# Differential projections ahead of the latent ones, and the output product of a hybrid attention block in Strassen's form

## The chip, the cores and the metric

One core of one Trainium2 chip runs the whole program. The metric is the device time of one execution in microseconds; the time of the kernel before is the median of three runs, 897.6 us (897.48 to 898.41).

## The reference

One decoder block over 1024 tokens with 1024 channels, all in float32. The input is normalised and projected; four heads of differential attention (two softmax maps, one subtracted from the other) and four heads of latent attention (queries and keys through low-rank projections) run on the same projection. What the change touches is the end:

```
merged = (jax.nn.sigmoid(g_diff) * (o_diff @ w_proj_diff[layer])
          + jax.nn.sigmoid(g_mla) * (o_mla @ w_proj_mla[layer]))
x = x + merged @ w_out[layer]
return rms_norm(x, norm_final)
```

Here `o_diff` and `o_mla` are 1024 x 512, the two projections 512 x 1024, `w_out` 1024 x 1024.

## The kernel before

Every product is made of matmuls on operands that are split in two parts, a rounded high part and the remainder as low part, so that a product of two float32 matrices is three matmuls of 512 columns (`mm3`, lines 159 to 162: high x high, high x low, low x high). `split` (lines 151 to 153) makes the two parts: a cast on ACT, then a subtraction on DVE or POOL.

The work is written down by Python generators. A generator yields the time that TensorE is thought to need; `fill`, `drain` and `drive` put pieces of one queue of generators between the steps of another, and `defer` and `flush` call a function once so many nanoseconds have been written down. From this order, the tiles' buffers and its own estimate of when an instruction can start, the framework sets each engine's final order: an instruction that it thinks is not yet ready is passed by later ones that are. On the chip each engine then takes its list strictly in that order, and SP's list of DMA issues too. A tile's buffer (a tag with so many `bufs`) is handed on when its last reader is through. PSUM has eight banks: four for scores, one each for `pv` and `tp`, and two under the tag `mm`, which the projections, the merge products and two of three transposes of the latent heads' values share (`tp_any`, line 760).

Ahead of the change stand the latent heads, h = 0 to 3, each with two groups of 512 queries: scores, softmax, transposes of the probabilities, values. Their loop is in lines 1030 to 1066. The places that the change touches are these.

- `merge_begin` (line 966) is called when head 2 is through. It opens the pool `p3a`, loads the four blocks of the differential output from `d_od` through one buffer of 128 x 1024 ("or"), splits each into `odh` and `odl` (line 974), and calls `load_p` twice.
- `load_p` (line 982) loads the next block of a projection weight (two buffers) and splits it with POOL; `p3["plan"]` holds their order.
- `product(br, j, done)` (line 995) is one merge product: for block j of 128 output channels and both halves of 512 tokens, 12 matmuls into a bank `mm`; branch 0 is differential, branch 1 latent. The gate's half tile `tg` is loaded from `d_t` (three buffers). `done_d` (line 1011) keeps the gated differential result in a tile `part`; `done_m` (line 1015) adds the latent one to it and splits the sum into `mh[j]`, `ml[j]`.
- When head 3 begins, pool `p3b` opens and products (0,0) and (0,1) are queued; `take` (line 1056) loads the latent output from `d_om` by halves through three buffers "omr" and splits it. These products stand between the steps of the last values, `mla_values(3, 1)`.
- Then products (1,j) and (0,j+2) alternate for j = 0 to 5, and (1,6), (1,7) follow (lines 1092 to 1096). `begin_out` loads and splits the first three blocks of `w_out`; the other five are loaded and split within the output stage.
- The output stage (line 1127 on) runs over the 8 blocks k of inner channels for the first four row blocks and both column halves, all eight banks in use, and then over row blocks 4 to 7 one at a time. `finish_half` adds the residual `x` and sums squares, `finish` scales the rows and stores them. The last row block is done in a half and two quarters of the columns, so that its finishing is short.

Of the kernel before, what the change touches and what calls it, by code (L numbers as in the profile page):

```python
# [23 lines left out]
P = 128  # L24
# [27 lines left out]
def emit(tc, a):  # L52
# [106 lines left out]
    def mm3(ps, lh, ll, rh, rl, first, last):  # L159
        T.matmul(ps, lhsT=lh, rhs=rh, start=first, stop=False)  # L160
        T.matmul(ps, lhsT=lh, rhs=rl, start=False, stop=False)  # L161
        T.matmul(ps, lhsT=ll, rhs=rh, start=False, stop=last)  # L162
# [801 lines left out]
    p3 = {}  # L964

    def merge_begin():
        pa = p3["a"] = pool("p3a", "right")
        p3["o"] = [[], []], [[], []]
        for k in range(4):
            r = mk(pa, [P, S], F32, "or", 1)  # L970
            nc.sync.dma_start(r, d_od[k])
            h_ = one(pa, [P, S], F32R, f"odh{k}")
            l_ = one(pa, [P, S], F32R, f"odl{k}")
            split(h_, l_, r)
            p3["o"][0][0].append(h_)
            p3["o"][0][1].append(l_)
        p3["w"] = deque()
        p3["plan"] = deque([(0, 0), (0, 1)] + [x for j in range(6) for x in ((1, j), (0, j + 2))] + [(1, 6), (1, 7)])
        for _ in range(2):
            load_p()  # L980

    def load_p():
        if p3["plan"]:
            br, j = p3["plan"].popleft()
            pa = p3["a"]
# [9 lines left out]
    def product(br, j, done):  # L995
        wh, wl = p3["w"].popleft()
        oh, ol = p3["o"][br]
        for n in range(2):
            t = mk(p3["a"], [P, 512], F32, "tg", 3)
# [30 lines left out]
    for h in range(4):  # L1030
# [17 lines left out]
        else:  # L1048
            pl2.release()
            pb = p3["b"] = pool("p3b", "right")  # L1050
            p3["o"][1][0].extend(one(pb, [P, S], F32R, f"omh{k}") for k in range(4))
            p3["o"][1][1].extend(one(pb, [P, S], F32R, f"oml{k}") for k in range(4))
            queue.append(product(0, 0, done_d))
            queue.append(product(0, 1, done_d))

            def take(k, n):
                r = mk(pb, [P, 512], F32, "omr", 3)
# [12 lines left out]

    p3c = pool("p3c", "left")
    mh = [one(p3c, [P, S], F32R, f"mh{j}") for j in range(8)]
    ml = [one(p3c, [P, S], F32R, f"ml{j}") for j in range(8)]
    EARLY = 3
    p3e = pool("p3e", "left")
    woh = [one(p3e, [P, D], F32R, f"woh{k}") for k in range(EARLY)]
    wol = [one(p3e, [P, D], F32R, f"wol{k}") for k in range(EARLY)]

    def load_out(k):
        wr = mk(p3e, [P, D], F32, "wor", 2)  # L1080
        nc.sync.dma_start(wr, a["w_out"][k])
        return wr

    def begin_out():
        raws = [load_out(k) for k in range(2)]
        split(woh[0], wol[0], raws[0])
        raws.append(load_out(2))
        split(woh[1], wol[1], raws[1])
        split(woh[2], wol[2], raws[2])

    defer(35000, begin_out)
    for j in range(6):
        queue.append(product(1, j, done_m))
        queue.append(product(0, j + 2, done_d))
    for j in (6, 7):
        queue.append(product(1, j, done_m))
# [3 lines left out]
    p3["a"].release()  # L1100

    p3d = pool("p3d", "right")
    nf = one(p3d, [P, D], F32, "nf")
    woh += [one(p3d, [P, D], F32R, f"woh{k}") for k in range(EARLY, KD)]
    wol += [one(p3d, [P, D], F32R, f"wol{k}") for k in range(EARLY, KD)]

    def load_res(b):
        xr = mk(p3d, [P, D], F32, "xres", 4)
        nc.sync.dma_start(xr, a["x"][b])
        return xr  # L1110

    def finish_half(xr, acc, s_, d):
        V.tensor_tensor(xr[:, half(d)], xr[:, half(d)], acc, op=ALU.add)
        junk = mk(p3d, [P, 512], BF16, "junk3", 1)
        A.activation(junk, xr[:, half(d)], AF.Square, accum_out=s_[:, d:d + 1])
        if d == 0:
            V.tensor_scalar(s_[:, 0:1], s_[:, 0:1], D * EPS, None, op0=ALU.add)

    def finish(b, xr, s_):
# [7 lines left out]
    ps.release()  # L1127
    ps3 = pool("ps3", space=PSUM)
    acc = [[mk(ps3, [P, 512], F32, "acc", 8) for d in range(2)] for q in range(4)]
    wos = deque(load_out(k) for k in (3, 4))  # L1130
    nc.sync.dma_start(nf, a["norm_final"].broadcast_to([P, D]))
    for k in range(KD):
        if k + 1 >= EARLY and k + 1 < KD:
            split(woh[k + 1], wol[k + 1], wos.popleft())
            if k + 3 < KD:
                wos.append(load_out(k + 3))
        for q in range(4):
            for d in range(2):
                mm3(acc[q][d], mh[k][:, blk(q)], ml[k][:, blk(q)], woh[k][:, half(d)], wol[k][:, half(d)],
                    k == 0, k == KD - 1)  # L1140
    res = [load_res(q) for q in range(4)]
    for q in range(4):
        s_ = mk(p3d, [P, 2], F32, "s3", 4)
        for d in range(2):
            finish_half(res[q], acc[q][d], s_, d)
        finish(q, res[q], s_)
    for b in range(4, NB - 1):
        xr = load_res(b)
# [111 lines left out]
```

## Time and profile before

| | |
|---|---|
| median of three runs | 897.6 us |
| the profiled execution's own time | 896.13 us |
| its span, first to last instruction | 894.4 us |
| between the two | 1.7 us |
| mean granted clock of TensorE | 0.995 |
| TensorE busy | 874.7 us, 98% |
| DVE, ACT, POOL busy | 538.5, 335.5, 219.5 us |

The page lists, for one profiled execution, how long each engine was busy, and 40 slices of the span. Times in the rows below are microseconds from the span's start. Durations of matmuls overlap (the next one starts before the last has drained), so the pace of TensorE is read from the distance of starts. A bracket at the end of a row tells how long the engine had stood before it and on what it waited.

### The profile page before, as it was taken

How to read it: one execution, taken by the hardware profiler on the slowest of the kernel's cores; microseconds unless marked ns; L12 is line 12 of the kernel's file. 1: busy time of each engine (PE TensorE's matmuls, PEld its weight loads, DVE VectorE, ACT ScalarE, POOL GpSimd, SP SyncE). 2: the span in 40 equal slices, each digit the busy share in tenths (PEclk: the TensorE clock that was granted, in tenths of full speed). 3: DMA queues.
4: the chain of work that ended last, by engine and by line, in shares of the span. 5: the costliest groups of instructions: out<-in, count | busy, mean ns of one | idle time of the engine just before them, and what ended most of it. 6: DMA issues, size and time to landing. Idle time of an engine off the chain costs nothing.

```text
span 894.4 us, 11691 instructions
## 1 busy us (share of the span) xinstructions
PE 874.7 (98%) x4368; PEld 716.0 (80%) x4368; DVE 538.5 (60%) x1023; ACT 335.5 (38%) x654; POOL 219.5 (25%) x163
## 2 busy tenths in 40 slices
PE   9989999999999999999999999999999999999997
PEld 6879988787887878878778778778877788888886
DVE  5472348738368483784856755786676775561432
ACT  5651361334323343233422333745455542221211
POOL 2432013222223222322223131622313212210001
PEclk9998999999999999999999999999999999999999
DMA  8765026122131222222211215410104655434151
GB/s 294 289 192 161 23 87 220 48 71 80 62 107 59 76 90 64 91 71 82 72 59 33 95 31 185 161 34 25 48 25 154 200 178 187 141 102 146 58 178 47
DMA packets 48824, 96.71 MB, mean 108 GB/s; under 512 B 4992, under 2 KB 17536, under 8 KB 48768
## 3 DMA queue, kind: packets, MB, share of 16 engines
q1 hardware_dynamic: 46176, 89.81, 30.4%
q0 software_dynamic: 1152, 3.67, 1.3%
q10 hardware_dynamic: 1440, 2.49, 0.8%
q8 instruction: 34, 0.56, 0.3%
q14 instruction: 22, 0.18, 0.1%
HBM read 68.96 MB, written 27.00 MB: 107 GB/s over the span
## 4 chain that ended last, share of the span: by engine, by line
PE 85%; DVE 4%; DMA 4%; issue 2%; ACT 2%; POOL 1%; SPq 1%; POOLq 0%; DVEq 0%; ACTq 0%
PE mm L160 18%; PE mm L162 17%; PE mm L161 17%; PE sc L619 4%; PE acc L160 3%; PE acc L161 3%; PE acc L162 3%; PE tp L457 2%; PE bank L161 2%; PE bank L160 2%; PE bank L162 2%; PE pv L161 2%; PE pv L160 2%; PE pv L162 1%; PE sc L898 1%
## 5 line engine op out<-in xcount | busy, mean ns | idle before, releaser
L160 PE MATMUL mm<-hh,wh 128*128 128x512 f32 x512 | 205.9, 402 | 0.0
L162 PE MATMUL mm<-hh,wl 128*128 128x512 f32 x512 | 200.2, 391 | 0.0
L161 PE MATMUL mm<-hl,wh 128*128 128x512 f32 x512 | 199.9, 390 | 0.0
L153 POOL TENSOR_TENSOR wl<-wr,wh 128x1024 fp32r<-128x1024 f32 x32 | 81.8, 2558 | 240.2 <-ACT wh L152 240.2
L160 PEld LDWEIGHTS mm<-hh,wh 128*128 128x128 f32 x512 | 96.2, 188 | 25.0 <-issue 3.8
L162 PEld LDWEIGHTS mm<-hh,wl 128*128 128x128 f32 x512 | 96.1, 188 | 21.2
L161 PEld LDWEIGHTS mm<-hl,wh 128*128 128x128 f32 x512 | 96.3, 188 | 17.9
L438 ACT ACTIVATE e<-sc,mn 128x128 f32<-128x128 f32 (+3 forms) x64 | 47.5, 743 | 82.9 <-DVE mn L435 80.0
L435 DVE CUSTOM_DVE_ANT_0 sc<-sc,mask 128x128 f32<-128x128 f32 (+7 forms) x96 | 71.7, 774 | 10.1 <-PE sc L902 8.7
L153 DVE TENSOR_TENSOR pl<-tp,ph 128x512 fp32r<-128x512 f32 (+2 forms) x52 | 31.5, 606 | 62.2 <-ACT ph L152 62.2
L152 ACT CAST ph<-tp 128x512 fp32r<-128x512 f32 (+2 forms) x52 | 27.0, 520 | 84.7 <-PE tp L457 84.2
L160 PE MATMUL acc<-woh,mh 128*128 128x512 f32 (+1 forms) x136 | 51.7, 380 | 0.0
L162 PE MATMUL acc<-woh,ml 128*128 128x512 f32 (+1 forms) x136 | 51.7, 380 | 0.0
L161 PE MATMUL acc<-wol,mh 128*128 128x512 f32 (+1 forms) x136 | 51.7, 380 | 0.0
L152 ACT CAST wh<-wr 128x1024 fp32r<-128x1024 f32 x32 | 33.6, 1050 | 39.0 <-PE mm L161 28.6
L160 PE MATMUL bank<-wch,hh 128*128 128x384 f32 (+1 forms) x128 | 42.7, 335 | 3.8 <-ACT wch L152 3.8
L911 POOL TENSOR_TENSOR e<-e,rs 128x128 f32<-128x128 f32 (+5 forms) x24 | 24.9, 1042 | 73.5 <-DVE rs L443 73.4
L161 PE MATMUL bank<-wcl,hh 128*128 128x384 f32 (+1 forms) x128 | 42.6, 333 | 0.3 <-DVE wcl L153 0.3
L569 DVE TENSOR_TENSOR g<-mm,rbc 128x512 f32<-128x512 f32 x40 | 27.5, 688 | 25.5 <-PE mm L162 25.0
L162 PE MATMUL bank<-wch,hl 128*128 128x384 f32 (+1 forms) x128 | 42.4, 331 | 0.0
L153 POOL TENSOR_TENSOR wpl<-wpr,wph 128x512 fp32r<-128x512 f32 x16 | 22.0, 1377 | 68.0 <-ACT wph L152 68.0
L572 ACT ACTIVATE u<-g 128x512 f32<-128x512 f32 x40 | 25.2, 630 | 20.3 <-DVE g L569 15.4
(291 smaller groups left out, 1859.0 us busy)
## 6 DMA issues: line engine op xcount, KB each, us to landing
wr<-in_w_t SPq DMA_DIRECT2D x32, 512.0 KB, 3.5
d_t<-u SPq DMA_DIRECT2D x32, 256.0 KB, 2.0
tg<-d_t SPq DMA_DIRECT2D x32, 256.0 KB, 3.0
big<-in_x SPq DMA_DIRECT2D x8, 512.0 KB, 8.3
wor<-in_w_out SPq DMA_DIRECT2D x8, 512.0 KB, 4.5
xres<-in_x SPq DMA_DIRECT2D x8, 512.0 KB, 5.1
big<-in_xT SPq DMA_DIRECT2D x7, 512.0 KB, 6.6
craw<-d_c SPq DMA_DIRECT2D x5, 512.0 KB, 6.0
```

The costliest lines, as they stand in the source:

```text
L152: A.copy(hi, src)
L153: (eng or V).tensor_tensor(lo, src, f32(hi), op=ALU.subtract)
L160: T.matmul(ps, lhsT=lh, rhs=rh, start=first, stop=False)
L161: T.matmul(ps, lhsT=lh, rhs=rl, start=False, stop=False)
L162: T.matmul(ps, lhsT=ll, rhs=rh, start=False, stop=last)
L435: V.tensor_tensor_reduce(sc[:, 0:W], sc[:, 0:W], mask[:, S - W:S], scale=-scale, scalar=BIG, op0=ALU.add, op1=ALU.min, accum_out=mn)
L438: A.activation(dst, sc[:, 0:W], AF.Exp, scale=-1.0, bias=mn, accum_out=sm)
L457: T.transpose(tp[:, blk(j)], probs[j][:, blk(kb)], ident)
L569: V.tensor_tensor(g, b, rbc[:, half(n)], op=ALU.mult)
L572: A.activation(u, g, AF.Tanh, scale=0.5 / by)
L619: T.matmul(sc[m][:, c0:c0 + n], lhsT=q[r, blk(i)], rhs=k[r, c0:c0 + n], start=x == 0, stop=x == 2)
L911: G.tensor_tensor(e, e, r.broadcast_to([P, W]), op=ALU.mult)
```

## The change

The latent and differential merge products no longer alternate: all eight differential ones come first, in the order of blocks 0, 4, 1, 5, 2, 6, 3, 7 (`JO`), then the eight latent ones in the same order. Pool `p3b` is opened already in `merge_begin`, and holds the latent output, the weights, the gates, `omr` (two buffers instead of three) and four `part` tiles; `p3a` holds only the differential output, which is now loaded in eight halves through one buffer of 128 x 512. `p3a` is given back between the two series. The merged matrix stays unsplit in `mr[j]`.

The output product is made as seven products of 512 x 512 x 512 (Strassen's form with Winograd's sums). `w_out` is loaded by blocks while the differential products run, and `weight_sums` makes its sums in place; `row_sums` makes those of `mr` on POOL while the latent products run. `prepare(n)` splits the operands of product n (left remainder on POOL, right on DVE) while product n - 1 runs; left operands have two sets of tiles, right ones three. `multiply(n, q)` is one row block of product n, 12 matmuls. Products 0, 2, 4, 5 gather in four banks, products 1, 3, 6 in the other four, and partial sums are added to the residual tiles, all eight of which are now loaded at the start. Row blocks 4 to 7 are finished after product 5, row blocks 0 to 3 after product 6, the last one in two quarters.

```diff
+        pb = p3["b"] = pool("p3b", "right")
+        p3["o"] = [[], []], [[], []]
...
+                                     ("omr", [P, 512], F32, 2), ("part", [P, 512], F32, 4)):
+            for _ in range(bufs):
+                mk(pb, shape, dt, tag, bufs)
         pa = p3["a"] = pool("p3a", "right")
-        p3["o"] = [[], []], [[], []]
         for k in range(4):
-            r = mk(pa, [P, S], F32, "or", 1)
-            nc.sync.dma_start(r, d_od[k])
             h_ = one(pa, [P, S], F32R, f"odh{k}")
             l_ = one(pa, [P, S], F32R, f"odl{k}")
-            split(h_, l_, r)
+            for n in range(2):
+                r = mk(pa, [P, 512], F32, "or", 1)
+                nc.sync.dma_start(r, d_od[k][:, half(n)])
+                split(h_[:, half(n)], l_[:, half(n)], r)
             p3["o"][0][0].append(h_)
             p3["o"][0][1].append(l_)
-        p3["plan"] = deque([(0, 0), (0, 1)] + [x for j in range(6) for x in ((1, j), (0, j + 2))] + [(1, 6), (1, 7)])
+        p3["plan"] = deque((br, j) for br in range(2) for j in JO)
...
     def done_d(j, n, t, b):
-        s_ = parts[j, n] = mk(p3["b"], [P, 512], F32, "part", 6)
+        s_ = parts[j, n] = mk(p3["b"], [P, 512], F32, "part", 4) if j in JO[0:2] else mr[j][:, half(n)]
         V.scalar_tensor_tensor(s_, t, 1.0, b, op0=ALU.add, op1=ALU.mult)
 
     def done_m(j, n, t, b):
         s_ = parts.pop((j, n))
         V.scalar_tensor_tensor(t, t, 1.0, b, op0=ALU.add, op1=ALU.mult)
-        V.tensor_tensor(t, t, s_, op=ALU.add)
-        split(mh[j][:, half(n)], ml[j][:, half(n)], t)
+        V.tensor_tensor(mr[j][:, half(n)], t, s_, op=ALU.add)
+        if n == 0:
+            left_operand(j // 4, j % 4, mr[j][:, half(0)])
+        elif j >= 4:
+            row_sums(j - 4)
...
             def take(k, n):
-                r = mk(pb, [P, 512], F32, "omr", 3)
+                r = mk(pb, [P, 512], F32, "omr", 2)
                 nc.sync.dma_start(r, d_om[k][:, half(n)])
                 defer(3500, lambda: split(p3["o"][1][0][k][:, half(n)], p3["o"][1][1][k][:, half(n)], r))
...
+    mr = [one(p3c, [P, S], F32, f"mr{j}") for j in range(8)]
+    ms1 = [one(p3c, [P, 512], F32, f"ms{i}") for i in range(4)]
...
+    def left_operand(n, i, src):
+        t = left_set[n, i] = mk(p3["s"], [P, 2, 512], F32R, f"a{n % 2}{i}", 1)
+        split(t[:, 0], t[:, 1], src, G if n > 1 else V)
+
+    def right_operand(n, i, src, eng=None):
+        t = right_set[n, i] = mk(p3["d"] if n % 3 == 2 else p3w, [P, 2, 512], F32R, f"b{n % 3}{i}", 1)
+        split(t[:, 0], t[:, 1], src, eng)
+
+    def row_sums(i):
+        a11, a12 = mr[i][:, half(0)], mr[i + 4][:, half(0)]
+        a21, a22 = mr[i][:, half(1)], mr[i + 4][:, half(1)]
+        G.tensor_tensor(ms1[i], a21, a22, op=ALU.add)
+        G.tensor_tensor(a21, a11, a21, op=ALU.subtract)
+        G.tensor_tensor(a11, ms1[i], a11, op=ALU.subtract)
+        G.tensor_tensor(a12, a12, a11, op=ALU.subtract)
+
+    def sub(eng, out, p_, q):
+        eng.tensor_tensor(out, p_, q, op=ALU.subtract)
+
+    def weight_sums(i):
+
+        b21, b22 = b2[i][:, half(0)], b2[i][:, half(1)]
+        right_operand(0, i, b11[i])
+        right_operand(1, i, b21)
+        sub(G, b11[i], b12[i], b11[i])
+        sub(V, b12[i], b22, b12[i])
+        sub(V, b21, b21, b22)
+        G.tensor_tensor(b21, b21, b11[i], op=ALU.add)
+
+    defer(1000, load_b1)
+    defer(6000, load_b2)
+    defer(11000, load_b12)
+    for i in range(4):
+        defer(18000 + 5000 * i, lambda i=i: weight_sums(i))
+    for j in JO[2:]:
+        queue.append(product(0, j, done_d))
+    drain()
+    flush()
+    p3["a"].release()
+    p3["s"] = pool("p3s", "left")
+    for j in JO:
         queue.append(product(1, j, done_m))
...
+    def prepare(n):
+        for i in range(4):
+            left_operand(n, i, (mr[i][:, half(0)], ms1[i], mr[i][:, half(1)], mr[i + 4][:, half(1)],
+                                mr[i + 4][:, half(0)])[n - 2])
+            if n == 2:
+                t2 = mk(p3d, [P, 512], F32, "t2", 2)
+                sub(V, t2, b2[i][:, half(1)], b11[i])
+                right_operand(2, i, t2)
+            else:
+                right_operand(n, i, (b11[i], b12[i], b2[i][:, half(0)], b2[i][:, half(1)])[n - 3])
...
+    def multiply(n, q, start):
+        bank_ = banks[n in (1, 3, 6)][q]
+        for i in range(4):
+            x, w = left_set[n, i], right_set[n, i]
+            mm3(bank_, x[:, 0, blk(q)], x[:, 1, blk(q)], w[:, 0], w[:, 1], start and i == 0, i == 3, not start)
+
+    def add(b, d, n, q):
+        V.tensor_tensor(res[b][:, half(d)], res[b][:, half(d)], banks[n][q], op=ALU.add)
...
+    def last_rows(q):
+
+        xr, s_ = res[q], stat[q]
+        V.tensor_scalar(s_[:, 0:1], s_[:, 0:1], D * EPS, None, op0=ALU.add)
+        G.tensor_tensor(xr[:, half(0)], xr[:, half(0)], nf[:, half(0)], op=ALU.mult)
+        quarters = (slice(0, 512), slice(512, 768), slice(768, 1024))
+        for i, bank_ in enumerate((banks[1][q], banks[0][q])):
+            p_ = slice(256 * i, 256 * i + 256)
+            c = quarters[1 + i]
+            for k in range(4):
+                x, w = left_set[6, k], right_set[6, k]
+                mm3(bank_[:, 0:256], x[:, 0, blk(q)], x[:, 1, blk(q)], w[:, 0, p_], w[:, 1, p_], k == 0, k == 3)
+            V.tensor_tensor(xr[:, c], xr[:, c], bank_[:, 0:256], op=ALU.add)
...
+    for n in range(7):
+        if 2 <= n + 1 < 7:
+            prepare(n + 1)
         for q in range(4):
+            if (n, q) == (6, 3):
+                last_rows(q)
+                continue
+            multiply(n, q, n in (0, 1, 3))
+            if n == 0:
+                add(q, 0, 0, q)
+            elif n == 1:
+                add(q, 0, 1, q)
+                if q < 3:
+                    squares(q, 0)
+                else:
+                    junk = mk(p3d, [P, 512], BF16, "junk3", 1)
+                    A.activation(junk, res[q][:, half(0)], AF.Square, accum_out=stat[q][:, 0:1])
+            elif n == 2:
+                add(q, 1, 0, q)
+            elif n == 3:
+                add(4 + q, 1, 1, q)
+                if q == 3:
+                    add(3, 1, 1, 3)
+            elif n == 4:
+                add(4 + q, 1, 0, q)
+                squares(4 + q, 1)
+            elif n == 5:
+                add(4 + q, 0, 0, q)
+                squares(4 + q, 0)
+                finish(4 + q)
+            else:
+                add(q, 1, 1, q)
+                squares(q, 1)
+                finish(q)
```

## Rows read from the trace of the kernel before

**Rows 1.** The page, part 1: busy us and share of the span of each engine.

```profile
PE 874.7 (98%) x4368; PEld 716.0 (80%) x4368; DVE 538.5 (60%) x1023; ACT 335.5 (38%) x654; POOL 219.5 (25%) x163
```

**Rows 2.** Busy time by windows: PE, PEld, DVE, ACT, POOL, then granted clock, DMA share, GB/s.

```profile
720.00:740.00 20.00, 20.00 (x95) 16.47 (x94) 14.35 (x19) 8.45 (x14) 4.40 (x3) 1.00 0.65 219
...
799.00:888.30 89.30, 89.30 (x410) 73.27 (x408) 30.70 (x55) 17.03 (x38) 5.90 (x9) 1.00 0.33 112
```

**Rows 3.** Instructions in order of time on PE, output stage: start, us, engine, line.

```profile
799.15 0.39 PE L160 MATMUL acc<-woh,mh 128*128 128x512 f32 x1
...
888.03 0.28 PE L162 MATMUL acc<-woh,ml 128*128 128x256 f32 x1
```

**Rows 4.** Groups of instructions by form, output stage.

```profile
L160 PE MATMUL acc<-woh,mh 128*128 128x512 f32 x120 | 47.2, 394 | 0.0
```

**Rows 5.** Order of time on PE: first and last of 21 and of 6 steps.

```profile
744.75 0.39 PE L160 MATMUL mm<-omh,wph 128*128 128x512 f32 x1
...
749.51 0.39 PE L160 MATMUL mm<-omh,wph 128*128 128x512 f32 x1
...
842.07 0.39 PE L160 MATMUL acc<-woh,mh 128*128 128x512 f32 x1
...
843.47 0.40 PE L160 MATMUL acc<-woh,mh 128*128 128x512 f32 x1
```

**Rows 6.** Tile omr, 690 to 725 us: durations ns min/median/max; DMA tg of the page.

```profile
L152 ACT CAST omh<-omr x7: 607/620/622, 704.9 to 715.8; 128x512 fp32r<-128x512 f32 x7
L153 DVE TENSOR_TENSOR oml<-omr,omh x7: 667/692/695, 705.8 to 716.4; 128x512 fp32r<-128x512 f32 x7
...
DMA to landing us min/median/max: 2.6/4.6/5.5
...
tg<-d_t SPq DMA_DIRECT2D x32, 256.0 KB, 3.0
```

**Rows 7.** Order of time on POOL.

```profile
734.93 1.82 POOL L153 TENSOR_TENSOR wpl<-wpr,wph 128x512 fp32r<-128x512 f32 x1 [3.88 <-ACT wph L152]
```

**Rows 8.** Order of time on SP's queue, and on DVE, 677 to 706 us.

```profile
677.63 0.39 SPq L971 DMA_DIRECT2D or<-d_od  x1
...
687.28 0.32 SPq L971 DMA_DIRECT2D or<-d_od  x1
...
699.05 0.32 SPq L971 DMA_DIRECT2D or<-d_od  x1
...
703.74 1.43 DVE L153 TENSOR_TENSOR odl<-or,odh 128x1024 fp32r<-128x1024 f32 x1
```

**Rows 9.** Tile or: time from issue to landing of its four loads.

```profile
DMA to landing us min/median/max: 3.2/3.6/4.8
```

**Rows 10.** Order of time on PE, from the first differential to the first latent product.

```profile
702.39 0.48 PE L160 MATMUL mm<-odh,wph 128*128 128x512 f32 x1
...
708.10 0.60 PE L457 MATMUL mm<-ident,e 128*128 128x128 f32 x4
...
722.49 0.39 PE L160 MATMUL mm<-omh,wph 128*128 128x512 f32 x1
```

**Rows 11.** Order of time on ACT.

```profile
690.93 1.05 ACT L152 CAST odh<-or 128x1024 fp32r<-128x1024 f32 x1 [1.68 <-DMA or<-d_od]
```

**Rows 12.** Order of time on DVE, end of the output stage.

```profile
877.08 0.69 DVE L1113 TENSOR_TENSOR xres<-xres,acc 128x512 f32<-128x512 f32 x1 [3.80 <-PE acc L162]
...
879.56 1.41 DVE L1124 SCALAR_TENSOR_TENSOR xres<-xres,r,nf 128x512 f32<-128x512 f32 x2 [0.73 <-POOL r L1122]
...
888.34 0.42 DVE L1168 TENSOR_TENSOR xres<-xres,acc 128x256 f32<-128x256 f32 x1 [1.63 <-PE acc L162]
```

**Rows 13.** PE in order of time, and a window (PE busy, granted clock), early.

```profile
61.98 0.33 PE L162 MATMUL bank<-wch,hl 128*128 128x384 f32 x1
66.11 0.69 PE L160 MATMUL bank<-wch,hh 128*128 128x384 f32 x1 [3.80 <-ACT wch L152]
...
71.00:72.00 1.00, 1.00 (x5) 0.50 0.93 221
```

More of the change, by code (lines that the diff above doesn't have):

```diff
@@ L157, in split_gain, with mm3 @@
         V.scalar_tensor_tensor(lo, src, gain, f32(hi), op0=ALU.mult, op1=ALU.subtract)
[L159 to L162, printed above, removed]
+    def mm3(ps, lh, ll, rh, rl, first, last, skip=False):
+        T.matmul(ps, lhsT=lh, rhs=rh, start=first, stop=False, skip_group_check=skip)
+        T.matmul(ps, lhsT=lh, rhs=rl, start=False, stop=False, skip_group_check=skip)
+        T.matmul(ps, lhsT=ll, rhs=rh, start=False, stop=last, skip_group_check=skip)
     def half(n):
@@ L1049, in emit @@
             pl2.release()
[L1050 to L1054, printed above, removed]
+            pb = p3["b"]
+            queue.append(product(0, JO[0], done_d))
+            queue.append(product(0, JO[1], done_d))
             def take(k, n):
-                r = mk(pb, [P, 512], F32, "omr", 3)
+                r = mk(pb, [P, 512], F32, "omr", 2)
                 nc.sync.dma_start(r, d_om[k][:, half(n)])
@@ L1071, in emit @@
     p3c = pool("p3c", "left")
[L1072 to L1095, printed above, removed]
+    mr = [one(p3c, [P, S], F32, f"mr{j}") for j in range(8)]
+    ms1 = [one(p3c, [P, 512], F32, f"ms{i}") for i in range(4)]
+    p3w = pool("p3w", "left")
+    left_set, right_set = {}, {}
+    b11 = [one(p3w, [P, 512], F32, f"b11_{i}") for i in range(4)]
+    b12 = [one(p3w, [P, 512], F32, f"b12_{i}") for i in range(4)]
+    b2 = [one(p3w, [P, D], F32, f"b2_{i}") for i in range(4)]
@@ new lines, in sub @@
+    def sub(eng, out, p_, q):
[11 more added lines that the diff above has]
+    defer(11000, load_b12)
+    for i in range(4):
+        defer(18000 + 5000 * i, lambda i=i: weight_sums(i))
@@ L1099, in emit @@
     p3["b"].release()
-    p3["a"].release()
-    p3d = pool("p3d", "right")
+    p3d = p3["d"] = pool("p3d", "right")
     nf = one(p3d, [P, D], F32, "nf")
[L1104 to L1113, printed above, removed]
-        junk = mk(p3d, [P, 512], BF16, "junk3", 1)
-        A.activation(junk, xr[:, half(d)], AF.Square, accum_out=s_[:, d:d + 1])
-        if d == 0:
-            V.tensor_scalar(s_[:, 0:1], s_[:, 0:1], D * EPS, None, op0=ALU.add)
@@ L1120, in finish, with squares @@
+    stat = [mk(p3d, [P, 3], F32, "s3", 8) for _ in range(NB)]
+    def squares(b, d):
+        junk = mk(p3d, [P, 512], BF16, "junk3", 1)
+        A.activation(junk, res[b][:, half(d)], AF.Square, accum_out=stat[b][:, d:d + 1])
+        if d == b // 4:
+            V.tensor_scalar(stat[b][:, d:d + 1], stat[b][:, d:d + 1], D * EPS, None, op0=ALU.add)
+    def finish(b):
+        xr, s_ = res[b], stat[b]
         V.tensor_scalar(s_[:, 1:2], s_[:, 1:2], s_[:, 0:1], 1.0 / D, op0=ALU.add, op1=ALU.mult)
@@ L1191, in emit @@
     ps3.release()
     p3d.release()
-    p3e.release()
+    p3["s"].release()
+    p3w.release()
     p3c.release()
```

109 lines of the change are left out of this document (45 added, 64 removed).

## The prediction

> **What bounds the kernel now.** First the page's head: TensorE is busy 98% of the span, no other engine above 60% [rows 1]. A busy PE may still wait between matmuls, so next the windows of the stretch that the change touches: in 720 to 740 us and in the output stage from 799 to 888 us PE has no free time and the granted clock is 1.00, while DVE has a quarter of it free or more, ACT and POOL over half [rows 2]. Third the starts of single matmuls, because their durations (0.39 us) overlap: the output stage runs from the start of its first matmul at 799.15 to 888.03 plus 0.12 for the last one, 89.0 us [rows 3]. It holds 360 matmuls of 512 columns (three code lines with 120 each, one of them in [rows 4]) and 48 of 256, together worth 384 of 512; 89.0 / 384 = 0.2318 us each. So here each matmul taken away is worth 0.23 us, unless PE then stands for something else. Ahead of it, from 722.49, PE runs the 14 remaining merge products without a gap. The stretch before that, 702 to 722 us, is the one in which PE does not run at its pace: 48 matmuls of the first two differential products and the last latent head's values stand there, and what feeds them is a chain of loads that the change alters.
>
> **The output stage.** Strassen's form does seven products of four row blocks x four inner blocks x three matmuls = 336 of 512 columns (the last twelve as 24 of 256) in place of 384. 48 x 0.2318 = 11.1 us less. The matmul has two paces in the trace: 21 steps take 4.76 us in the merge products (0.2267 each), 6 steps 1.40 us late in the output stage (0.2333) [rows 5]. All 336 at the fast pace are 76.2 us (12.8 saved), at the slow one 78.4 (10.6 saved). I take the stage's own mean, 11.1.
>
> **What the seven products need, and its cover.** One product lasts 48 x 0.2318 = 11.1 us. Preparing the next one takes eight ACT casts of 0.62, four DVE subtractions of 0.69 [rows 6] and four on POOL. POOL's subtraction of this size took 1.82 us beside a busy DVE [rows 7], the most in this stretch: 4 x 1.82 = 7.3. ACT has 5.0 us, and 8.3 with the four squares; DVE 5.5 with four additions of 0.69, 8.3 where T2 is built. Only in product 5 DVE is over: its four row blocks are finished too (4 x (0.69 + 1.41 + 0.36); the 1.41 of the scalings stands in the row cited for the tail), 12.6 us with product 6's subtractions, which come first in order; 1.5 us of finishing slip into product 6, whose own are 9.8. The rest stands beside PE. The left operands have two sets, so product n+1's can be written once product n-1 is through: a whole product of 11.1 us for a chain of 0.62 + 7.3. Cost nothing; gone if POOL needed over 2.6 us per operation.
> The early work is hidden too. The six differential products that are left after 722 last 6 x 24 x 0.2267 = 32.6 us; the weight sums put 16 x 0.69 = 11 us on DVE and 8 x 1.82 = 15 on POOL there. The row sums (16 x 1.82 = 29 us on POOL) lie within the eight latent products, 43.5 us; the last four end about 0.7 + 0.7 + 7.3 = 8.7 us into the first Strassen product and are first needed after it. w_out's 4.2 MB now come within the 32.6 us, with 12 gate halves and 8 weight blocks 9.4 MB, 288 GB/s, where 720 to 740 us moved 219 [rows 2]: gate loads land later, but the matmul that would wait for one stands two halves (5.4 us) behind. Nothing, with up to 2 us if a gate load falls behind the 2 MB of one burst. Putting all differential products first changes only the order of 14 products that ran without a gap.
>
> **The chain that feeds the first product.** This is the part that I charge. merge_begin loads d_od as four tiles of 512 KB through one buffer: load, cast, subtract, then the next load. SP issues at 677.63, 687.28 and so on to 699.05; the fourth subtraction ends at 703.74 + 1.43 = 705.17 [rows 8]. The two last periods are 5.9 us: 3.6 to land [rows 9], and cast and subtraction. The first differential matmul starts at 702.39 [rows 10], so PE hardly waits for it. After the change there are eight halves through one half-size buffer. A link is 2.9 (256 KB; 2.6 at least, 4.6 the median beside others) + 0.62 + 0.69 + 0.1 = 4.3 us [rows 6]; a link is not half as long as before, because landing does not halve. The second issue comes between 677.6 + 4.3 = 682 and 687.3 as now; I take 685. The first half product needs the seventh half (block 3, left half): 685 + 6 x 4.3 = 710.8 us instead of 705.2.
> What stands behind it: in order of emission the first half product and then the second hold both buffers of the "mm" tag, and the first transposes of the last values take such a buffer too. They ran at 708.10 [rows 10]; now they follow at 710.8 + 0.7 (three matmuls) + 0.7 (done_d) + 0.1 = 712.3: 4.2 late. Until then PE can do only the 18 matmuls whose blocks are in (4.2 us). What comes after is the same work, 14.4 us up to 722.49 before, and two matmuls more (0.5 us, since 23 of the 48 were done by 708.10); six further differential products are ready by then as filler for the waits in it, for which I take back 1 us (0 to 2, an estimate). Charge: 4.2 + 0.5 - 1 = 3.7, say 4 us. Ends: links of 3.9 us from 682 give 705.4, no charge; links of 6 us from 687.3 give 723.3, 18 us.
> ACT takes its queue in order: at 690.93 a cast of this chain stood 1.68 us for its load [rows 11] with the values' casts behind it. Eight such casts instead of four, each for half the bytes, and the omr loads through two buffers instead of three: 0.5 us (0 to 1.7).
>
> **The tail.** In the last row the finishing of a block now comes every 2.8 us of PE instead of 5.6. Before, block 6's scaling pair ran from 2.5 to 3.9 us after its addition, at 879.56 against 877.08, long before the last addition at 888.34 [rows 12]. Now that pair of block 2 lies from T+2.8 to T+4.2 after its last matmul, and the last addition of block 3 is due at T+3.2. DVE delays it by up to 1.1, and by what is left of the 1.5 us: 1.0 us (0 to 2). The rest of the tail is as before.
>
> **Sum.** -11.1 + 4.0 + 0.5 + 1.0 = -5.6 us. The span of 894.4 becomes 888.8, the profiled execution of 896.13 becomes 890.5; the median of the runs was 897.6, 1.5 above the profiled one, so the forecast is 892.0.
>
> **The clock.** When PE stood from 61.98 to 66.11 the granted clock was 0.50 afterwards, the lower level of 1.2 GHz, and still so from 71 to 72 us [rows 13]: some 6 us at half speed, 3 us lost. My gap is broken by single matmuls and transposes (the longest piece is 2.8 us), and in 720 to 740 the clock was 1.00, so I charge none. The Trainium skill, "TensorE: Matmul & The Clock Gate", Part 1, "What's actually happening", has the throttled state as the default, which activity releases; [rows 13] agree. If that struck here, the sum would be -2.6 and the time 895.0.
>
> **Rivals.**
> - The chain keeps up: links near 3.9 us, or the order of the engines' work gives PE enough beside it. Then -11.1 + 0.5 + 1.0 = -9.6, 888.0 us; with the fast pace 886.3. For it: DMA moves 256 KB in 2.6 us at best [rows 6]. Against: the chain is serial, and omr loads run beside its second half.
> - Slower: the chain and the omr loads, now both through buffers that must be emptied first, block each other in SP's and ACT's queues. At 6 us a link the seventh half is there at 723.3 and the transposes at 724.8, 16.7 late. -11.1 + 16.7 + 0.5 - 1 + 0.5 + 1.0 + 3 (the clock, PE standing for long) = +9.6, 907 us. It decides from about 5.3 us a link (716.8), where charge and tail eat the gain. For it: omr's median of 4.6 us to land and SP in order. Against: the two last periods before held no time beyond landing, cast and subtraction.
> - The operands bind the output stage: at 3.5 us per POOL operation the chain is 0.62 + 14 = 14.6, 3.5 more than a product, for the four products 3 to 6: +14 on the sum, 906 us. Against: 1.82 is the most seen.
>
> **How the numbers follow.** The forecast 0.53 (888.5 to 896); the chain keeps up 0.25; the blocked chain 0.08; operands 0.04; 0.10 for something between forecast and blocked chain, clock included, 896 to 901. The runs before differ by 0.1%, so a change under 0.2% (895.8 to 899.4) cannot be told from none. Faster: 0.51 + 0.25 + 0.04 = 0.80; within 0.2%: 0.02 of the forecast's and 0.06 of the between; slower: the two rivals' 0.12. Range 885.5 to 897.0: from full gain at the fast pace to a charge of some 9 us; about 0.1 lies on either side.
>
> **What would show it.** The output stage from first to last matmul at 76 to 79 us with no gap between products: right on the main term; gaps of a microsecond ahead of each product with PE waiting for POOL's subtraction: the operand rival. The eight d_od loads should be issued some 4.3 us apart, the transposes of the last values begin near 712, and PE stand 5 to 7 us in all from 702 to 715. A seventh half in before 706 makes my charge wrong; one after 717 makes the forecast wrong. The last addition should start about 1 us later behind its matmul than the 0.3 us of now.

## The result and the profile after

The changed kernel takes 906.69 us (median of 4 runs, 904.53 to 909.83) where the kernel before, run beside it, takes 897.54 (897.19 to 898.41): ratio 1.0103, 95% interval 1.0071 to 1.0136. It is slower, and outside the range that was given. The profiled executions are 907.61 and 896.13 us, their spans 905.9 and 894.4: 11.5 us to be found.

The program is the same up to the merge, so the span is cut there, by starts of TensorE instructions: the first differential matmul (1); from it to the last matmul of the latent values, by which 48 or 49 of the 192 differential matmuls have run in every kernel (2, the front); from there to the first output matmul (3, the rest of the products); the output stage up to the start of its last matmul (4); the rest (5, the end).

| profiled run | 1 start | 2 front | 3 products | 4 output | 5 end | span |
|---|---|---|---|---|---|---|
| before | 702.39 | 20.57 | 76.19 | 88.88 | 6.37 | 894.4 |
| after | 700.77 | 29.96 | 87.06 | 76.87 | 11.24 | 905.9 |
| difference | -1.6 | +9.4 | +10.9 | -12.0 | +4.9 | +11.5 |

The start varies from 699.4 to 703.3 among kernels that do not differ ahead of it, so experiments are read by stage, and spans only together with their runs' medians. A stage is that of one profiled execution, which can lie some microseconds from the median of its kernel's runs.

First the output stage: TensorE in order of time, then a window (PE, PEld, DVE, ACT, POOL busy; granted clock; DMA share; GB/s); they answer to [rows 2, 3].

```profile
817.79 0.39 PE L160 MATMUL acc<-b,a 128*128 128x512 f32 x1
...
894.66 0.28 PE L162 MATMUL acc<-b,a 128*128 128x256 f32 x1
```

```profile
818.00:894.80 76.80, 76.80 (x348) 63.39 (x346) 58.26 (x80) 31.44 (x68) 41.46 (x31) 1.00 0.27 96
```

76.87 us and no idle time: Strassen's seven products give what the count of matmuls says, and their operands are always there in time.

From 695 us up to it TensorE has six waits of over 0.6 us. In order of time, with what ended each wait (these answer to [rows 10]):

```profile
706.83 0.49 PE L160 MATMUL mm<-odh,wph 128*128 128x512 f32 x1 [1.45 <-ACT odh L152]
...
711.43 0.80 PE L160 MATMUL mm<-odh,wph 128*128 128x512 f32 x1 [3.15 <-ACT odh L152]
...
714.16 1.11 PE L457 MATMUL mm<-ident,e 128*128 128x128 f32 x4 [0.78 <-DVE part L1023]
...
716.00 0.80 PE L160 MATMUL pv<-ph,mvh 128*128 128x512 f32 x1 [0.73 <-ACT ph L152]
...
747.60 0.79 PE L160 MATMUL mm<-odh,wph 128*128 128x512 f32 x1 [3.08 <-DVE mr L1023]
...
758.80 0.50 PE L160 MATMUL mm<-odh,wph 128*128 128x512 f32 x1 [2.78 <-DVE mr L1023]
```

Four are the front, with the loads of d_od and what follows from them; two lie among the differential products and wait for done_d on DVE (L1023). The windows of the same stretches (columns as above) show what each stop brings with it:

```profile
708.00:712.00 4.00, 0.85 (x3) 0.29 (x1) 1.28 (x2) 1.82 (x3) 0.00 (x0) 0.62 0.62 199
712.00:716.00 4.00, 2.49 (x7) 1.21 (x6) 2.15 (x5) 1.28 (x4) 0.00 (x0) 0.50 0.70 229
716.00:720.00 4.00, 4.00 (x11) 3.07 (x12) 3.03 (x5) 2.10 (x4) 0.19 (x1) 0.60 0.07 26
...
744.00:748.00 4.00, 0.92 (x4) 0.50 (x3) 3.96 (x6) 0.62 (x1) 1.79 (x2) 0.82 0.78 284
748.00:752.00 4.00, 4.00 (x10) 3.06 (x10) 2.83 (x4) 0.00 (x0) 3.84 (x4) 0.50 0.61 205
752.00:756.00 4.00, 4.00 (x15) 2.89 (x13) 1.57 (x2) 0.62 (x1) 4.00 (x4) 0.83 0.01 2
756.00:760.00 4.00, 1.22 (x6) 1.03 (x6) 3.34 (x4) 0.00 (x0) 4.00 (x3) 1.00 0.05 10
760.00:764.00 4.00, 4.00 (x12) 3.12 (x12) 0.69 (x1) 0.62 (x1) 1.03 (x2) 0.57 0.58 187
```

The granted clock is 0.50 to 0.60 behind each of the three longest stops, 0.50 being the 1.2 GHz level: 10 to 12 matmuls in 4 us of a busy PE where some 18 belong (4 / 0.2267). Busy time times the missing share of the clock is 3.2 us from 708 to 720 and 4.6 us from 744 to 764. At the two stops among the differential products DVE is busy where PE is idle (3.96 and 3.34 of 4 us), and DVE's order shows with what:

```profile
737.00 3.56 DVE L153 TENSOR_TENSOR b<-b,b 128x512 fp32r<-128x512 f32 x4
740.49 0.67 DVE L1023 SCALAR_TENSOR_TENSOR mr<-tg,mm 128x512 f32<-128x512 f32 x1
741.09 0.68 DVE L153 TENSOR_TENSOR b<-b,b 128x512 fp32r<-128x512 f32 x1
741.80 0.69 DVE L1128 TENSOR_TENSOR b<-b 128x512 f32<-128x512 f32 x1
...
746.27 0.68 DVE L153 TENSOR_TENSOR b<-b,b 128x512 fp32r<-128x512 f32 x1
746.87 1.28 DVE L1023 SCALAR_TENSOR_TENSOR mr<-tg,mm 128x512 f32<-128x512 f32 x2
...
751.59 0.69 DVE L1128 TENSOR_TENSOR b<-b,b 128x512 f32<-128x512 f32 x1 [1.17 <-POOL b L1128]
754.71 3.44 DVE L1128 TENSOR_TENSOR b<-b,b 128x512 f32<-128x512 f32 x2 [2.43 <-POOL b L1128]
758.07 1.27 DVE L1023 SCALAR_TENSOR_TENSOR mr<-tg,mm 128x512 f32<-128x512 f32 x2
```

From 737.00 to 746.87 DVE does splits (L153) and subtractions (L1128) of w_out's blocks with no gap over 0.15 us, and one done_d among them; the two done_d that TensorE's banks wait for stand behind. Then subtractions wait for POOL, and two done_d again stand behind.

Last the end, on DVE, to be held against [rows 12]:

```profile
879.28 0.68 DVE L1190 TENSOR_TENSOR xres<-xres,acc 128x512 f32<-128x512 f32 x1
880.81 0.21 DVE L1202 TENSOR_SCALAR s<-s 128x1 f32<-128x1 f32 x1 [0.85 <-ACT junk L1196]
881.70 1.42 DVE L1206 SCALAR_TENSOR_TENSOR xres<-xres,r,nf 128x512 f32<-128x512 f32 x2 [0.67 <-POOL r L1204]
883.03 0.68 DVE L1190 TENSOR_TENSOR xres<-xres,acc 128x512 f32<-128x512 f32 x1
...
899.78 0.41 DVE L1221 TENSOR_TENSOR xres<-xres,acc 128x256 f32<-128x256 f32 x1
```

Addition, wait for ACT's square, wait for POOL's factor, scaling, next addition: 3.75 us, while TensorE has a block ready every 2.8 us. The last addition starts 5.1 us behind its matmul (0.3 in [rows 12] and the last start of [rows 3]).

### The profile page after: what moved, and what is told of

Same layout as the page of the kernel before. It is cut to its first block, busy times and chain, and to the rows that moved or that the text cites. A ratio compares the mean times of both kernels' runs of the same rounds, so it can differ in the third digit from the quotient of the medians.

```text
span 905.9 us, 11737 instructions
## 1 busy us (share of the span) xinstructions
PE 870.4 (96%) x4308; PEld 709.7 (78%) x4308; DVE 580.5 (64%) x1064; ACT 349.1 (39%) x690; POOL 286.9 (32%) x207
## 4 chain that ended last, share of the span: by engine, by line
PE 80%; DVE 7%; DMA 6%; ACT 2%; issue 2%; POOL 2%; SPq 0%; POOLq 0%; DVEq 0%; ACTq 0%
PE mm L160 18%; PE mm L162 17%; PE mm L161 17%; PE sc L619 4%; PE acc L160 2%; PE acc L162 2%; PE acc L161 2%; PE tp L457 2%; PE bank L161 2%; PE bank L160 2%; PE bank L162 2%; PE pv L161 2%; PE pv L160 2%; PE pv L162 2%; DMA big<-in_xT 1%
## 5 line engine op out<-in xcount | busy, mean ns | idle before, releaser
L153 POOL TENSOR_TENSOR wl<-wr,wh 128x1024 fp32r<-128x1024 f32 x32 | 81.8, 2557 | 240.2 <-ACT wh L152 240.2
L153 DVE TENSOR_TENSOR pl<-tp,ph 128x512 fp32r<-128x512 f32 (+2 forms) x52 | 31.5, 606 | 63.9 <-ACT ph L152 63.8
L161 PE MATMUL acc<-b,a 128*128 128x512 f32 (+1 forms) x116 | 44.5, 383 | 0.0
L160 PE MATMUL acc<-b,a 128*128 128x512 f32 (+1 forms) x116 | 44.4, 383 | 0.0
L162 PE MATMUL acc<-b,a 128*128 128x512 f32 (+1 forms) x116 | 44.4, 383 | 0.0
L569 DVE TENSOR_TENSOR g<-mm,rbc 128x512 f32<-128x512 f32 x40 | 27.5, 687 | 25.5 <-PE mm L162 25.0
L153 POOL TENSOR_TENSOR wpl<-wpr,wph 128x512 fp32r<-128x512 f32 x16 | 21.2, 1323 | 67.6 <-ACT wph L152 62.7
L160 PE MATMUL mm<-odh,wph 128*128 128x512 f32 x64 | 28.0, 443 | 10.4 <-DVE mr L1023 5.9
```

Of the source, the lines that this page charges most:

```text
L153: (eng or V).tensor_tensor(lo, src, f32(hi), op=ALU.subtract)
L160: T.matmul(ps, lhsT=lh, rhs=rh, start=first, stop=False, skip_group_check=skip)
L161: T.matmul(ps, lhsT=lh, rhs=rl, start=False, stop=False, skip_group_check=skip)
L162: T.matmul(ps, lhsT=ll, rhs=rh, start=False, stop=last, skip_group_check=skip)
L569: V.tensor_tensor(g, b, rbc[:, half(n)], op=ALU.mult)
```

## The experiments

All but one kernel are the changed kernel with the edit named. Ratios are to the kernel before, run beside them.

**The front: the kernel before with the loads in halves.** 1.0087 (1.0062 to 1.0112).

```
-            r = mk(pa, [P, S], F32, "or", 1)
-            nc.sync.dma_start(r, d_od[k])
+            for n in range(2):
+                r = mk(pa, [P, 512], F32, "or", 1)
+                nc.sync.dma_start(r, d_od[k][:, half(n)])
...
```

> The kernel before, with nothing changed but the loading of d_od: eight halves through one half-size buffer in place of four tiles through one. Theory A (the chain of eight short links is slower than that of four long ones and alone makes TensorE stand at the first product): the seventh half is cast near 708 to 712 where the fourth tile was cast near 703, TensorE stands 3 to 6 us between 700 and 716 with its clock down to half behind it, and the time is 4 to 9 us above the kernel before. Rival A' (the loss comes from the new order of the work that follows): the change is under 2 us.

Its front is 31.29 us for 20.57, all other stages are as before (76.21, 88.88, 6.64). TensorE:

```profile
708.58 0.49 PE L160 MATMUL mm<-odh,wph 128*128 128x512 f32 x1 [1.37 <-ACT odh L152]
...
713.23 0.80 PE L160 MATMUL mm<-odh,wph 128*128 128x512 f32 x1 [3.19 <-ACT odh L152]
```

The same two stops as in the changed kernel, in a kernel with nothing else of the change. In this execution the half-size buffer alone costs 10.7 us of the span. The execution took 907.30 us and was the slowest of its four (the others 903.14 to 903.90), so by the medians it costs less, 903.64 against 896.77: 6.9 us. The order of the products costs nothing visible there: the kernels with the changed kernel's front have 29.7 to 31.0 us in this stage.

**Left halves first.** 903.28 us, 1.0068 (1.0049 to 1.0088). The loop over n is put outside the loop over k.

> The eight loads of d_od now bring the four left halves first and then the four right ones, so the first half product needs the fourth link of the chain and not the seventh; nothing else is altered. Theory A (the seven links before the first product, with the clock that falls while TensorE stands, are what the front loses): the fourth left half is cast near 695 to 698 us, TensorE gets to its first differential matmuls by 700 and does not stand from 706 to 716, the granted clock stays above 0.9 from 700 to 722, and the time is 6 to 10 us below the changed kernel's 906.7, near 898. Rival A' (the front loses by the new order of all the work, whatever the order of the loads): TensorE still stands some 5 us there and the time moves by under 2 us.

A partial miss: the front falls by 3.8 us to 26.17 and the median by 3.4, where 6 to 10 us of time were expected. The first half product no longer waits for the seventh load, but the second one needs all eight, whose last cast is at 714.42, and TensorE stops there instead (715.09, for 2.02 us). Order only moves a stop if the chain stays as long.

**Three buffers.** 897.10 us, 1.0008 (0.9990 to 1.0026).

```
-                r = mk(pa, [P, 512], F32, "or", 1)
+                r = mk(pb, [P, 512], F32, "omr", 2) if (2 * k + n) % 3 else mk(pa, [P, 512], F32, "or", 1)
```

> The changed kernel, with the eight halves of d_od taken in turn through three buffers that exist already (the one of the chain and the two of the latent rows' loads, which are idle until then); no byte is added. Theory A: three loads in flight make the chain some 12 to 15 us long, the eighth half is cast before 698, TensorE does not stand between 700 and 720, its granted clock stays above 0.95 there, and 8 to 10 us are saved against the changed kernel's 906.7: 897 to 899. More than with the left halves first (3.4 us), which moved the stop behind to the right halves. Rival (the latent rows' loads, now late, make a stop of their own at the first latent product or hold SP's queue): under 4 us saved.

The front is 19.48 us, one less than before the change, with no clock lost:

```profile
708.00:712.00 4.00, 4.00 (x20) 3.29 (x21) 2.60 (x5) 2.14 (x4) 1.06 (x1) 1.00 0.68 227
712.00:716.00 4.00, 4.00 (x22) 3.08 (x21) 2.75 (x5) 1.73 (x3) 0.00 (x0) 1.00 0.56 192
716.00:720.00 4.00, 4.00 (x22) 2.94 (x21) 2.76 (x5) 2.14 (x5) 1.28 (x1) 1.00 0.03 9
```

So it was the depth of one, not the halves. The latent rows' loads, which now come later, make no stop.

**The two stops among the differential products.** What these products take beyond 0.2267 us per matmul, below called the pace (stage 3 up to the first latent matmul, less the matmuls left) is 11.0 us in the changed kernel. Three kernels take it apart.

```
# loads and sums spread by inner block
-    defer(1000, load_b1)
-    defer(6000, load_b2)
-    defer(11000, load_b12)
+    def load_b(i):
+        nc.sync.dma_start(b11[i], a["w_out"][i][:, half(0)])
+        defer(2000, lambda: nc.sync.dma_start(b2[i], a["w_out"][4 + i]))
+        defer(4000, lambda: nc.sync.dma_start(b12[i], a["w_out"][i][:, half(1)]))
...
-        defer(18000 + 5000 * i, lambda i=i: weight_sums(i))
+        defer(1000 + 6000 * i, lambda i=i: load_b(i))
+        defer(10000 + 6000 * i, lambda i=i: weight_sums(i))
# all sums on DVE
-        sub(G, b11[i], b12[i], b11[i])
+        sub(V, b11[i], b12[i], b11[i])
...
-        G.tensor_tensor(b21, b21, b11[i], op=ALU.add)
+        V.tensor_tensor(b21, b21, b11[i], op=ALU.add)
# no sums: those two lines and the two subtractions between them are left out,
# so the last five products multiply raw blocks
```

> w_out's twelve loads of this step come as three for each inner block, 2 us apart, every 6 us, and each block's weight sums 9 us behind its first load, instead of three bursts of four; the bytes and the sums are the same. Theory B1 (the gate load that landed 8.8 us after its issue stood behind the burst): no stop of 3 us near 744, the granted clock there stays near 1.00, gate loads land in under 5 us, 3 to 5 us saved for that stop alone. The sums themselves also come singly, so the DVE queue waits for POOL in four short pieces rather than one long one; if that alone makes the second stop (755.6 to 758.8, theory B2), it goes too and 7 to 11 us are saved in all, near 897 to 899. Rival (the loads compete for bandwidth, not for a place in the queue): gate loads land in 6 us or more still, in more places, and under 2 us are saved.

> The two of the four weight sums that POOL did are done by DVE, so no instruction of DVE waits for POOL there; DVE gets 8 x 0.69 = 5.5 us more work. Theory B2 (the second stop, 755.63 to 758.80, is DVE standing at its subtraction until POOL has ended, with the next done_d behind it): that stop goes, the granted clock after 760 stays near 1.00, and 3 to 6 us are saved, 901 to 904; the first stop at 744 stays. Rival (DVE is simply too full in this stretch): with more work on it the stop grows, and the time is the same or up to 4 us more.

> The changed kernel without the four sums of w_out's blocks (so the last five products use raw blocks); all loads stay in their bursts, and the splits of the first two weight operands stay. It tells apart the two readings of the first stop in the differential products (744.1 to 747.6): the gate load that was issued at 737.12 in the middle of the burst landed at 745.9, and DVE, which was busy without a gap from 737.0, came to the same done_d at 746.87. B1 (the landing binds): done_d still cannot start before about 9 us behind that load's issue, a stop of 2.5 us or more stays, and the first to last differential matmul takes about 69 us. B3 (DVE's queue binds: splits and subtractions of the burst stand ahead of done_d): the stop falls under 1 us and the stretch takes 66 or less. Either way the second stop is gone.

| | us | ratio (95%) | beyond the pace |
|---|---|---|---|
| spread | 901.47 | 1.0053 (1.0035 to 1.0072) | 2.7 |
| sums on DVE | 905.21 | 1.0085 (1.0057 to 1.0113) | 6.3 |
| no sums | 900.07 | 1.0047 (1.0032 to 1.0062) | 1.5 |

With the sums on DVE the second stop goes and the first stays (2.99 us at 750.14), as B2 said; the stage gains 4.8 us, while the medians differ by 1.5 of the 3 to 6 expected (its profiled run starts the stage 2.6 us later). With the spread the longest waits left there are 0.86 and 0.56 us. Its median gains 5.2 us of the 7 to 11 expected, and its profiled run (898.45) is among the fastest of ten that reach 903.95, so the other runs lost more somewhere; no trace shows where. The kernel without sums was to tell what the first stop was. Its gate loads, with all bursts in place:

```profile
DMA to landing us min/median/max: 2.5/2.8/9.3
```

and TensorE's only wait of over half a microsecond there:

```profile
745.98 0.50 PE L160 MATMUL mm<-odh,wph 128*128 128x512 f32 x1 [0.93 <-DVE mr L1023]
```

A gate load still lands up to 9.3 us after its issue, but the stretch from the first to the last differential matmul takes 63.4 us, not 69. My own first reading of the trace after, that the gate load behind the burst made this stop (B1), falls as the whole cause: DVE's queue (B3) held done_d last. It stays as a part. In the changed kernel the gate of the done_d at 746.87 was issued at 735.27 and landed 9.9 us later, at 745.2. TensorE had stood since 744.5, and its next matmul starts 0.73 us after the start of done_d. With the landing alone the stop would thus have been some 1.4 us (an estimate from these times); DVE's queue added the other 1.7.

In the kernel with three buffers the two lie further apart. TensorE and DVE there:

```profile
739.31 0.62 PE L160 MATMUL mm<-odh,wph 128*128 128x512 f32 x1 [5.00 <-DVE mr L1023]
```

```profile
738.58 1.27 DVE L1023 SCALAR_TENSOR_TENSOR mr<-tg,mm 128x512 f32<-128x512 f32 x2
```

The gate of this done_d was issued at 724.32 and landed 9.1 us later, 5.2 us before done_d began, while DVE did splits and subtractions: here the whole stop is DVE's queue.

The stop that is left without sums is a little longer than B3 had it (1.3 us from start to start, not under 1). The gate of its done_d landed at 744.4 and done_d began at 745.25, behind two splits; so it is DVE's queue again.

**The end: less work on DVE, or another order.** The first kernel lets POOL and ACT scale one half of each block ("scaling shared"): 907.42 us, 1.0119 (1.0095 to 1.0143). The second makes the scaling of block b depend on the addition of the next block: 903.39 us, 1.0077 (1.0056 to 1.0098).

```
# scaling shared
+            G.tensor_tensor(res[b][:, half(d)], res[b][:, half(d)], nf[:, half(d)], op=ALU.mult)   # in squares
...
+            if d == b // 4:
+                A.activation(xr[:, half(d)], xr[:, half(d)], AF.Identity, scale=r_, bias=0.0)
...
# behind the next addition (finish is called one block later, its factor made ahead)
+        V.scalar_tensor_tensor(r_, res[nxt][:, c:c + 1], 0.0, factor[b], op0=ALU.mult, op1=ALU.add)
```

> In the output stage the half of a row block that is final early is multiplied by the norm weights on POOL when its squares are taken, and ACT scales it in finishing; DVE does one scaling pair fewer, 0.7 us per block. Theory C2 (the tail is DVE's load: additions late from product 5 on because finishing fills it): the last addition starts under 2 us after its matmul instead of 5.0 and the end behind the last matmul falls from 11.1 to 8 us or less; 2.5 to 4 us saved, 903 to 904. Theory C1 (it is the order: each finishing waits on DVE for ACT's square and POOL's sum, with the next addition behind it): the wait of about 1.8 us per block stays, and under 1.5 us are saved.

> In the last two products a row block's scaling pair is made to come behind the next block's addition in DVE's queue (its factor passes through a one-column instruction that reads that addition's result); no other work moves, DVE has 7 one-column instructions more. Theory C1 (the tail is the order: addition, ACT's square, POOL's factor and scaling stand in a row of 3.75 us on DVE where PE has a block ready every 2.75): additions of the sixth product start within 1 us of their matmuls, the last one under 2 us behind its own instead of 5.0, and the stretch from the last matmul's start to the end falls from 11.2 to 7 or 8 us: 3 to 4 us saved, 903 to 904. Theory C2 (the load), for which the sharing of the scaling already spoke against it: nothing is saved, and 1 us lost by the extra instructions.

DVE with the scaling shared, and then with the scaling behind the next addition:

```profile
880.04 0.75 DVE L1210 SCALAR_TENSOR_TENSOR xres<-xres,r,nf 128x512 f32<-128x512 f32 x1 [2.74 <-POOL r L1205]
...
883.74 0.68 DVE L1190 TENSOR_TENSOR xres<-xres,acc 128x512 f32<-128x512 f32 x1
885.21 0.21 DVE L1203 TENSOR_SCALAR s<-s 128x1 f32<-128x1 f32 x1 [0.79 <-ACT junk L1196]
886.09 0.75 DVE L1210 SCALAR_TENSOR_TENSOR xres<-xres,r,nf 128x512 f32<-128x512 f32 x1 [0.66 <-POOL r L1205]
886.76 0.68 DVE L1190 TENSOR_TENSOR xres<-xres,acc 128x512 f32<-128x512 f32 x1
```

```profile
880.17 0.69 DVE L1190 TENSOR_TENSOR xres<-xres,acc 128x512 f32<-128x512 f32 x1 [0.27 <-PE acc L162]
880.97 0.16 DVE L1212 SCALAR_TENSOR_TENSOR r<-xres,r 128x1 f32<-128x1 f32 x1
881.16 1.41 DVE L1214 SCALAR_TENSOR_TENSOR xres<-xres,r,nf 128x512 f32<-128x512 f32 x2
882.50 0.21 DVE L1204 TENSOR_SCALAR s<-s 128x1 f32<-128x1 f32 x1
```

Shared, DVE has less to do and still waits twice per block, one block every 3.02 us, and the end stays at 10.92 us (11.24). That is no clean verdict on DVE's load: the first block's factor comes 2.74 us late, because POOL does the new multiplication ahead of it, and this alone puts DVE some 2 us behind at the start. What decides is the other order, in which DVE has no less to do. There the same pair of scalings stands where DVE has time, the additions wait for TensorE again, and the end is 8.10. It was the order (C1).

**The edits together.** Three buffers, spread loads, scaling behind the next addition; then with all weight sums on DVE; with the scaling shared; with both.

> Three edits in one: d_od through three buffers, w_out's loads and sums spread by inner block, scaling behind the next addition. If the three theories hold and the pieces are independent, the gains add up: about 9 for the front, 8 for the differential products (65.1 us from first to last differential matmul were seen with the spread loads where 73.2 stood), 3.5 for the tail, 20 in all, 885 to 888 us, 1.0 to 1.4% faster than the kernel before. If they take from one another (a stop that one removes only shows the next), 890 to 896.

> The kernel of the three edits, with all weight sums on DVE. If what is left in its differential products (55.4 us, against 52.8 without any stop) comes from DVE waiting for POOL and from slow instructions beside POOL (1.4 to 1.7 us where 0.69 stands alone), it falls by 1 to 2 us, 886 to 887. If DVE's load is what is left, the 8 additional instructions (5.5 us) cost 1 to 3 us: 889 to 891.

> The kernel of the three edits, with the early half of each block's scaling moved from DVE to POOL (norm weights) and ACT (factor). In the tail DVE does one scaling, not a pair, between the last row's statistics and its own scaling: the 8.1 us from the last matmul's start to the end become 7.2 to 7.5, time 886.5 to 887.5. Where ACT, which now scales ahead of the next square, or POOL gets late, nothing is gained or up to 1 us lost.

> Both of the two kernels above in one: the three edits, all weight sums on DVE, the scaling shared. If both gain, 885 to 886.5; if the sums on DVE cost, 888 to 890.

| | us | ratio (95%) | front | beyond the pace | end |
|---|---|---|---|---|---|
| three edits | 887.93 | 0.9904 (0.9883 to 0.9926) | 19.90 | 3.3 | 8.12 |
| and sums on DVE | 884.42 | 0.9875 (0.9859 to 0.9892) | 19.62 | 0.25 | 8.46 |
| and scaling shared | 887.72 | 0.9911 (0.9896 to 0.9925) | 19.39 | 3.2 | 7.43 |
| and both | 884.35 | 0.9875 (0.9860 to 0.9889) | 19.46 | 0.26 | 7.38 |

The gains add up, and the waits that are left among the differential products with the three edits (0.60, 0.30 and 0.85 us) go only when POOL has no weight sums: 3 us, more than the 1 to 2 expected. Sharing the scaling shortens the end by 0.7 and 1.1 us, which the medians do not show. With the three edits and the sums on DVE the change is 1.25% faster than the kernel before.

## Why the prediction was wrong

**The output stage was right.** -11.1 was said, -12.0 came, inside the bounds; no gap between products, so the rival by which the operands bind falls.

**"The early work is hidden too" is the step that failed:** it was costed at "nothing, with up to 2 us", and stage 3 lost 10.9. The sum of durations was not what failed first: 11 us of DVE within 32.6 does fit, beside 12 done_d. It left out that DVE works in order: a done_d behind ten microseconds of such work holds a bank, and TensorE with it. The sum was short too: beside POOL's sums, DVE's 16 splits and subtractions took 16.2 us instead of 11. Without the sums the stage loses 1.5 us, in small pieces 2.7, in small pieces and without POOL 0.25 (in the kernel with the three edits). The slow gate load was foreseen, with up to 2 us, and is there; by itself it would have cost some 1.4 us at the first stop.

**The front was right in place and wrong in size.** The seventh half was due at 710.8; its cast ends at 711.38 and the matmul behind it starts at 711.43, and TensorE's waits from 702 to 715 add up to 5.8 us where 5 to 7 were said. That the time of the seventh half came out was luck: the second load went out at 681.52 instead of 685, and from there six links took 5.1 us each (4.5 to 6.8) instead of 4.3. Transposes "near 712": 714.16. From them to the last value matmul the same work was to take 0.5 us more and get 1 back; it took 16.57 us instead of 14.86. Those two terms (the transposes 6.1 us later than before, and 1.7) make the 7.8 us by which the front ends later (9.4 with its earlier start) where 3.7 stood. The step "so I charge none" for the clock failed: the granted clock fell to 0.50 across a gap broken by single matmuls, 3.2 us by the windows, close to the 3 us named and set aside. The three matmuls ahead of the first done_d lasted from 711.43 to 713.38, where 0.7 us stood. And the further products were no filler for the chain: each half product needs all four blocks of d_od (the loop over k in `product`), so none could be finished before the seventh half, while TensorE stood 1.45 and 3.15 us. What the shared queue of ACT cost (0.5 was charged) could not be told apart from this.

**The tail, "1.0 us (0 to 2)", was 4.9.** DVE's work was added up; the waits for ACT and POOL inside the chain of one block (0.85 + 0.67 us) were not, and a chain of 3.75 us every 2.8 piles up over seven blocks, to the 5.1 us of the last addition. Placed by order alone, 1.7 us of it are left.

The sum without these terms holds: with the front, the sums and the tail mended, 12.0 gained in the output stage comes out as 884.4 against 895.8 in the same runs, 11.4 us. The slower rival named the front's chain but not the two places on DVE. Its 907 us is near the measured 906.69 by luck: it had the seventh half at 723.3, which came at 711.4, and it gave the products nothing and the tail 1 us. In the chances, 0.04 of the case between forecast and blocked chain was counted as faster, though its 896 to 901 lies wholly above 895.8.

## What to carry to other kernels

Work moved into the cover of a busy TensorE is hidden only if each engine's queue is: before costing it at nothing, list what stands behind it in order on that engine, and who waits for that. Where one engine waits for two others within each item, compare the length of that chain with the pace of items, not the engine's sum of durations, and put the next item's first step ahead of the wait. A buffer halved in size with a depth of one makes a chain half as long again (here 41.6 us from the first issue to the last subtraction, where 27.5 stood); look for idle buffers of the same shape, as the latent rows' two were here.

## What the runs showed of the hardware

DVE and POOL slow each other when both work from SBUF, where the tiles lie. In the kernel with three buffers, POOL and DVE at the weight sums at the same time (DVE first, then POOL):

```profile
740.38 6.85 DVE L1128 TENSOR_TENSOR b<-b,b 128x512 f32<-128x512 f32 x4
```

```profile
741.55 3.43 POOL L1128 TENSOR_TENSOR b<-b,b 128x512 f32<-128x512 f32 x2
```

1.71 us for each DVE subtraction, and as much for POOL's, which take 1.29 in the changed kernel where DVE stands (at 753.38). In the kernel of the three edits with the sums on DVE the DVE subtractions take 0.68, and done_d, with one operand from PSUM, takes 0.67 to 0.69 in either:

```profile
734.34 0.68 DVE L1128 TENSOR_TENSOR b<-b,b 128x512 f32<-128x512 f32 x1
734.95 0.68 DVE L1128 TENSOR_TENSOR b<-b 128x512 f32<-128x512 f32 x1
735.55 0.67 DVE L1023 SCALAR_TENSOR_TENSOR mr<-tg,mm 128x512 f32<-128x512 f32 x1
```

So the 0.69 used for DVE's subtractions in the prediction did not hold beside POOL's sums. Moving POOL's eight sums to DVE cost DVE little: its 16 splits and subtractions take 17.7 us in the kernel of the three edits, and the 24 of the kernel with all sums on DVE take 18.3. The Trainium skill has this in "SBUF — State Buffer", "Who interferes with whom": a DVE instruction with two SBUF inputs contends with a GpSimd instruction that reads SBUF. The traces agree.

Beside w_out's 4 MB, issued from 730.48 to 741.95 in the changed kernel, three gate loads of 256 KB in the same queue land 5.9 to 9.9 us after their issue (the median of the stretch is 2.9); with the same bytes issued over 24 us, up to 6.1. Whether the place in the queue or the bandwidth makes it was not told apart.
